# A decoder layer on one core: single rows' products and value products issued in unbroken groups, and the single rows of two projections' second halves moved behind the first row block

## The chip, the cores and the metric

The kernel runs on one core of a Trainium2 chip. A core has a matrix engine (TensorE, PE in the profile), whose weight loads are shown apart (PEld), a vector engine (VectorE, DVE), a scalar engine (ScalarE, ACT), a general engine (GpSimd, POOL) and an engine that here only issues transfers (SyncE, SP). Each engine takes its own instructions strictly in the order in which they were written down for it; between engines there are semaphores. The metric is the device time of one execution in microseconds. Before the change it is 970.07 us (median of three, 969.19 to 971.19).

## The reference, cut to what matters

One layer of a hybrid decoder serves a prompt of 512 rows and a group of 32 single rows (8 sequences of 4 tokens) with the same weights. The prompt attends to itself; the single rows attend to cached tokens and to cached memory of their own.

```python
h = rms_norm(x, g_mix_pre); z = h @ w_in             # mixer: 4 mLSTM heads, 4 differential attention heads
...
x = x + rms_norm(mix @ w_out, g_mix_post)
x = x + rms_norm(mem_attend(rms_norm(x, g_mem_pre), mk, mv, w_mq, w_mo), g_mem_post)   # 256 memory tokens
f, conv_new = conv_ffn(rms_norm(x, g_ffn_pre), conv_buf, w_up, w_dw, b_dw, w_down)     # gated MLP
x = x + rms_norm(f, g_ffn_post)
...
past_k = cache_dk[l][page_table]; past_v = cache_dv[l][page_table]   # single rows: 256 cached tokens each
ys, ... = layer(ys, pos_s, attend_s, ..., cache_mem_k[l], cache_mem_v[l], ...)
```

The model width is 1024, there are 4 heads of 256 in the attention to memory, and the MLP is 2752 wide.

## The kernel before, in words

The 544 rows are four row blocks b0 to b3 of 128 prompt rows and a fifth block, called 4 in the code, of the 32 single rows. All is float32; the big products of the prompt rows take their operands split into a high part (a cast on ACT, L142) and a low part (what the cast lost, a subtraction on DVE or POOL, L143), and three matmuls for each product: high by high (L387), high rows by low weights (L388), low rows by high weights (L389).

The single rows use full float32 in one product instead. A block of 32 rows fills 32 of the array's 128 columns, so `sample_mm` (L367) issues four matmuls at a time into four column groups that run side by side, each on other rows of the weights or on other output columns. It reads the weights from the staging tile in which they came from memory (`wst`, six buffers), not from the split copy (`wslot`, four slots). The profile counts two records for each such float32 matmul. The products of the single rows with cached memory and cached tokens work in the same way: scores against memory (`ssc`, L1396), values of cached tokens (`ops`, L1251), values of memory (`pso`, L1413); there each column group is a head.

A slot and its staging tile live as follows. SP loads 512 KB into `wst`; ACT casts it into the slot's high half as soon as the slot is free, and DVE then makes the low half. A staging tile can be loaded again only when both the split and the single rows' product have read it.

Two projections, `w_out` and `w_mo`, are computed in two halves of 512 output columns each (`proj_add`). The second half goes block by block with all four slots held (`block_major` in `gemmA`): one block takes 8 products of three matmuls. When a block is done, its row sums of squares, its scaling and its addition to the residual follow (`ev1`), its result is written to memory, and the next block's old residual `xb` is loaded. In the half-way point of each block, `mid` may transpose an earlier block's normalised rows (tile `tp`) into the next matmul's operand (`hqT` behind `w_out`, `fT` behind `w_mo`).

The program is traced once in Python; a scheduler then sets the order in which each engine gets its instructions, by dependences, its own cost model and priorities. So instructions that stand together in the code can be pulled apart: those of the single rows serve as filling wherever the scheduler believes that nothing else is ready. `tc.issue_after(x)` puts a block's instructions behind x on x's engine, and `tc.high_priority()` lets the scheduler prefer them.

Names in the prediction: "singles" are the 16 matmuls (32 records) that the single rows take for one half of a projection; a "run" is a number of column-group matmuls with nothing else of PE between them.

Of the kernel before, what the change touches and what calls it, by code (L numbers as in the profile page):

```python
# [1 line left out]

# [13 lines left out]
P = 128  # L16
DM = 1024
SEQ = 512
NB = 8
TS = 4  # L20
NS = NB * TS
ROWS = SEQ + NS
H = 4
# [50 lines left out]
def kernel(ctx: ExitStack, tc: tile.TileContext, I, O):  # L74
# [38 lines left out]
    def mmp(name="mm"):  # L113
        return psm.tile([P, 512], F32, name=name, tag="mm")
# [11 lines left out]
    mm = nc.tensor.matmul  # L126
# [200 lines left out]

    allb = [0, 1, 2, 3, 4]

    class Fill:  # L330


# [42 lines left out]
    def gemmA(xt, nk, blocks, evac, block_major=False, before=None, mid=None):  # L375


        ps = {}

        def one(b, k, s):  # L380
            if b == 4:
                if k % 2 == 0:
                    sample_mm(ps[b], [xt.sam(k), xt.sam(k + 1)], s[1], k == 0, k == nk - 2)
                return
            s, kk = s[0], k % 2
            c0, n = rows(b)
            mm(ps[b], lhsT=xt.hi(k, c0, c0 + n), rhs=s[:, 0, kk, :], start=(k == 0), stop=False)  # L387
            mm(ps[b], lhsT=xt.hi(k, c0, c0 + n), rhs=s[:, 1, kk, :], start=False, stop=False)  # L388
            mm(ps[b], lhsT=xt.lo(k, c0, c0 + n), rhs=s[:, 0, kk, :], start=False, stop=(k == nk - 1))  # L389

        if block_major:
            slots = [W.get() for _ in range((nk + 1) // 2)]
            for b in blocks:
                if before:
                    before(b)
                ps[b] = mmp()
                for k in range(nk):
                    if k == MIDK and mid:
                        mid()
                    one(b, k, slots[k // 2])  # L400
                    if b == blocks[-1] and k % 2 == 1:
                        W.free()
                evac(b, ps[b])
                yield 5.1
        else:
            for b in blocks:
                ps[b] = mmp()
            behind = []
            for k in range(nk):
                if k % 2 == 0:  # L410
                    s = W.get()
                    if 4 in blocks:
                        behind.append((k, s))
                for b in blocks:
                    if b < 4:
                        one(b, k, s)
# [211 lines left out]
    for c0, c1 in HALF:  # L628
        n = c1 - c0
        ps = mmp()  # L630
# [436 lines left out]
    def proj_add(xt, gname, src, gname2, dst, order=None, scale=None):  # L1067
# [173 lines left out]
    vts = {}  # L1241
# [4 lines left out]
            gather("cache_dv", b, g, st[:, 512 * g:512 * g + 512])  # L1246

    def dv_out(b):
        for g in range(2):
            for h in range(H):  # L1250
                mm(ops[NS * h:NS * h + NS, :P], lhsT=az[g][:, h, b * NS:(b + 1) * NS],  # L1251
                   rhs=vts[b][:, g * 512 + h * P:g * 512 + (h + 1) * P], start=(b == 0 and g == 0), stop=False)

    for t, _ in enumerate(pipe(NB, dv_load, lambda b: None, dv_out)):
        if t % 2 == 0:
# [133 lines left out]
            (VCP if q else nc.scalar.copy)(out=kts[b][:, 4 * q:4 * q + 4, c * P:(c + 1) * P], in_=v2(ps, P))  # L1389
        return t.ins  # L1390

    def mk_scores(b):
        ps = mmp("ssc")[:, :256]
        for c in range(2):
            for h in range(H):
                t = mm(ps[NS * h:NS * h + NS], lhsT=qs[:, 2 * h + c], rhs=kts[b][:, 2 * h + c, :], start=(c == 0), stop=(c == 1))  # L1396
        sample_exp(sall, b, ps, nm, su)
        return t.ins

    def mv_load(b):  # L1400

# [5 lines left out]
        for c in range(2):  # L1407
            dma(out=vts[b][c], in_=I["cache_mem_v"][0, b, c * P:(c + 1) * P].rearrange("t h d -> t (h d)"))

    def mv_out(b):  # L1410
        for c in range(2):
            for h in range(H):
                t = mm(pso[NS * h:NS * h + NS], lhsT=az[c][:, h, b * NS:(b + 1) * NS], rhs=vts[b][c][:, 256 * h:256 * h + 256],  # L1413
                       start=(b == 0 and c == 0), stop=(b == NB - 1 and c == 1))
        return t.ins

    sall = S([P, NB, 256], F32, "cas")
    nm, su = small(NB, "snm"), small(NB, "ssu")
# [8 lines left out]
                mk_load(j + 6)  # L1427

    next(prompt)
    for b in range(4):  # L1430
        t = mk_scores(b)
    with tc.issue_after(t):
        for j in range(8, 16):
            t = mk_turn(j)
# [5 lines left out]
        mv_load(b)  # L1440
    next(prompt)
    with tc.issue_after(t):
        for b in range(4, NB):
            t = mk_scores(b)
    for b in range(3, 7):
        mv_load(b)
    next(prompt)
# [4 lines left out]
    for n0 in (0, 512):  # L1452
        slotsA(w_mo, n0)
    W.nslots = NSLOT
    for b in range(4):
        mv_out(b)
        if b == 0:
            mv_load(7)
    W.pump()
    next(prompt, None)  # L1460
    next(prompt, None)
    for b in range(4, NB):
        mv_out(b)
    run(prompt)
    oS = Z("oS")[:, :256]
    nc.scalar.copy(out=oS, in_=pso)
# [357 lines left out]
```

## Time and profile before

| | |
|---|---|
| median of three runs | 970.07 us |
| profiled execution | 968.01 us, of which 966.2 us are its span |
| mean granted TensorE clock | 0.989 of full speed |
| PE busy | 940.1 us of the span |
| ACT, DVE, POOL busy | 388.0, 598.6 and 202.6 us |

The profile is one execution. In a timeline a row gives the start, the duration, engine, line, operation, output and inputs; "x8" says that eight neighbouring records of one kind are put together, and the bracket at its end how long the engine stood idle before it and what ended the wait. On PE, neighbouring matmuls overlap in the records, so that the distance from one start to the next tells what a matmul costs, not its duration.

### The profile page before, as it was taken

What the parts mean: (1) busy time and instruction counts of PE and PEld (TensorE: products, weight loads), DVE (VectorE), ACT (ScalarE), POOL (GpSimd) and SP (SyncE); (2) the same over time, 40 slices, a digit from 0 to 9 for tenths busy, and PEclk for the clock granted to TensorE, in tenths of its full rate; (3) what the DMA queues carried; (4) which work ended last, traced back from release to release, by engine and by line L of the source; (5) the groups of instructions that cost most, each with busy time, mean ns of one, the idle gap of its engine ahead of it and who ended that gap; (6) DMA issues with size and microseconds to landing.
All of it is one profiled execution on the core that took longest, in us unless ns stands there. A gap on an engine that the chain in (4) does not pass through costs nothing.

```text
span 966.2 us, 17070 instructions
## 1 busy us (share of the span) xinstructions
PE 940.1 (97%) x6615; PEld 813.3 (84%) x6615; DVE 598.6 (62%) x1127; ACT 388.0 (40%) x746; POOL 202.6 (21%) x397
## 2 busy tenths in 40 slices
PE   8999999999999999999999799999999999999994
PEld 5999787779866788998767699989988997997983
DVE  6835145555786367625554759827758675675677
ACT  6744134343686367534533524332212222222232
POOL 6610000016332124200000544301110110110114
PEclk9999999999999999999999999999999999999997
DMA  9950024344835359846734844063053303503213
GB/s 303 299 160 1 1 88 134 88 126 133 256 100 173 133 180 322 258 144 209 287 133 128 229 138 128 4 174 89 5 142 79 120 25 91 150 25 90 86 48 114
DMA packets 120529, 130.27 MB, mean 135 GB/s; under 512 B 8551, under 2 KB 85960, under 8 KB 120448
## 3 DMA queue, kind: packets, MB, share of 16 engines
q1 hardware_dynamic: 114264, 125.69, 41.9%
q10 hardware_dynamic: 6184, 3.48, 1.2%
q8 instruction: 52, 0.85, 0.4%
q14 instruction: 29, 0.24, 0.1%
HBM read 112.22 MB, written 16.93 MB: 134 GB/s over the span
## 4 chain that ended last, share of the span: by engine, by line
PE 86%; DVE 4%; DMA 4%; ACT 2%; POOL 2%; issue 1%; SPq 0%; DVEq 0%; POOLq 0%; ACTq 0%
PE mm L451 32%; PE mm L439 8%; PE mm L387 6%; PE mm L389 6%; PE mm L388 6%; PE mm L1660 4%; PE mm L1659 4%; PE mm L1658 4%; PE mm L367 2%; PE tpk L1388 1%; PE sda L1183 1%; DMA xb<-in_x_prompt_dram 1%; DMA wst<-in_w_mo_dram 1%; PE sca L1339 1%; DVE wslot L143 1%
## 5 line engine op out<-in xcount | busy, mean ns | idle before, releaser
L451 PEld LDWEIGHTS mm<-fT,wslot 128*128 128x128 f32 x1872 | 234.3, 188 | 2.1 <-issue 1.2
L451 PE MATMUL mm<-fT,wslot 128*128 128x256 f32 (+1 forms) x1872 | 236.0, 288 | 0.0
L142 ACT CAST wslot<-wst 128x1024 fp32r<-128x1024 f32 x125 | 131.1, 1051 | 254.7 <-PE mm L451 76.0
L143 DVE TENSOR_TENSOR wslot<-wst,wslot 128x1024 fp32r<-128x1024 f32 x125 | 155.7, 1249 | 90.9 <-ACT wslot L142 90.9
L1659 PE MATMUL mm<-wslot,act 128*128 128x512 f32 x176 | 69.6, 396 | 0.0
L1660 PE MATMUL mm<-wslot,act 128*128 128x512 f32 x176 | 68.9, 397 | 0.0
L1658 PE MATMUL mm<-wslot,act 128*128 128x512 f32 x176 | 68.7, 392 | 0.0
L1565 POOL COPY cvo<-u 128x2 f32<-128x2 f32 x43 | 15.2, 354 | 201.2 <-DVE u L1563 191.2
L387 PE MATMUL mm<-wslot,hT 128*128 128x512 f32 x128 | 52.2, 408 | 0.0
L388 PE MATMUL mm<-wslot,hT 128*128 128x512 f32 x128 | 51.3, 401 | 0.0
L389 PE MATMUL mm<-wslot,hT 128*128 128x512 f32 x128 | 51.3, 402 | 0.0
L1560 DVE TENSOR_TENSOR u<-mm,rsb 128x256 f32<-128x256 f32 x43 | 18.2, 424 | 52.9 <-PE mm L451 50.9
L451 PE MATMUL mm<-hT,wslot 128*128 128x256 f32 (+1 forms) x384 | 51.0, 289 | 0.0
L451 PEld LDWEIGHTS mm<-hT,wslot 128*128 128x128 f32 x384 | 49.2, 188 | 0.8 <-issue 0.4
L1658 PEld LDWEIGHTS mm<-wslot,act 128*128 128x128 f32 x176 | 33.6, 191 | 8.6 <-issue 0.8
L1659 PEld LDWEIGHTS mm<-wslot,act 128*128 128x128 f32 x176 | 33.1, 188 | 7.2
L1660 PEld LDWEIGHTS mm<-wslot,act 128*128 128x128 f32 x176 | 33.1, 188 | 7.2
L1577 ACT ACTIVATE c<-c 128x560 f32<-128x560 f32 x21 | 14.1, 672 | 54.9 <-DVE c L1571 51.6
L1571 DVE SCALAR_TENSOR_TENSOR c<-u,cvT,c 128x560 f32<-128x560 f32 x43 | 34.2, 796 | 0.8
L1570 DVE SCALAR_TENSOR_TENSOR c<-u,cvT,c 128x560 f32<-128x560 f32 x43 | 34.1, 792 | 0.1
L439 PE MATMUL mm<-fT,wslot 128*128 128x256 f32 (+1 forms) x192 | 27.2, 303 | 2.6 <-POOL fT L143 2.4
L1671 DVE TENSOR_TENSOR yp<-mm,yp 128x512 f32<-128x512 f32 x40 | 27.1, 687 | 3.9 <-PE mm L1660 3.8
(469 smaller groups left out, 1868.3 us busy)
## 6 DMA issues: line engine op xcount, KB each, us to landing
wst<-in_w_up_dram SPq DMA_DIRECT2D x42, 512.0 KB
wst<-in_w_in_dram SPq DMA_DIRECT2D x28, 512.0 KB
wst<-in_w_down_dram SPq DMA_DIRECT2D x20, 512.0 KB
wst<-in_cache_mem_k_dram SPq DMA_DIRECT2D x16, 512.0 KB
wst<-in_w_mk_dram SPq DMA_DIRECT2D x8, 512.0 KB
xb<-in_x_prompt_dram SPq DMA_DIRECT2D x8, 512.0 KB
wst<-in_cache_dk_dram SPq DMA_DIRECT2D x16, 256.0 KB
wst<-in_cache_dv_dram SPq DMA_DIRECT2D x16, 256.0 KB
```

The lines of the kernel that those rows point to most:

```text
L142: nc.scalar.copy(out=hi, in_=src)
L143: (eng or nc.vector).tensor_tensor(out=lo, in0=src, in1=f32(hi), op=SUB)
L387: mm(ps[b], lhsT=xt.hi(k, c0, c0 + n), rhs=s[:, 0, kk, :], start=(k == 0), stop=False)
L388: mm(ps[b], lhsT=xt.hi(k, c0, c0 + n), rhs=s[:, 1, kk, :], start=False, stop=False)
L389: mm(ps[b], lhsT=xt.lo(k, c0, c0 + n), rhs=s[:, 0, kk, :], start=False, stop=(k == nk - 1))
L439: mm(ps, lhsT=s[:, l, k, :], rhs=x(k, c0, c1), start=(k == 0 and j == 0), stop=(k == 7 and j == 2))
L451: mm(ps[i], lhsT=s[:, l, k, :], rhs=x(k, c0, c1), start=(k == 0 and j == 0), stop=(k == 7 and j == 2))
L1570: STT(out=c, in0=u[:, 1:EXT - 1], scalar=w[1], in1=c, op0=MUL, op1=ADD)
L1571: STT(out=c, in0=u[:, 0:EXT - 2], scalar=w[0], in1=c, op0=MUL, op1=ADD)
L1658: mm(ps, lhsT=t[:, 0, c0:c0 + P], rhs=s[:, 0, i % 2, :], start=st, stop=False)
L1659: mm(ps, lhsT=t[:, 0, c0:c0 + P], rhs=s[:, 1, i % 2, :], start=False, stop=False)
L1660: return mm(ps, lhsT=t[:, 1, c0:c0 + P], rhs=s[:, 0, i % 2, :], start=False, stop=en)
```

## The change

A small context manager `burst(ins)` is added: nothing for `None`, otherwise behind `ins` on its engine with high priority. With it

- the singles are issued behind the last row block's last product in the plain form of `gemmA`, and behind the previous block's last product in its block-major form;
- the second halves of `w_out` and `w_mo` go in the order b0, 4, b1, b2, b3 instead of 4, b0, b1, b2, b3 (and the loads of `xb` with them);
- the value products over cached tokens (`dv_out`) are issued for two sequences at a time, each behind the one before;
- the scores (`mk_scores`) and the value products (`mv_out`) over cached memory are chained in the same way, the latter in pairs for the second four sequences.

```diff
+    @contextmanager
+    def burst(ins):
+        if ins is None:
+            yield
+        else:
+            with tc.issue_after(ins), tc.high_priority():
+                yield
...
         if block_major:
             slots = [W.get() for _ in range((nk + 1) // 2)]
+            t = None
             for b in blocks:
                 if before:
                     before(b)
                 ps[b] = mmp()
+                if b == 4 and t is not None:
+                    with burst(t.ins):
+                        for k in range(nk):
+                            one(b, k, slots[k // 2])
+                    evac(b, ps[b])
+                    yield 2.1
+                    continue
                 for k in range(nk):
                     if k == MIDK and mid:
                         mid()
-                    one(b, k, slots[k // 2])
+                    t = one(b, k, slots[k // 2])
...
             if behind:
-                for k, s in behind:
-                    one(4, k, s)
+                with burst(t.ins):
+                    for k, s in behind:
+                        one(4, k, s)
                 evac(4, ps[4])
...
-            run(gemmA(xt, 8, [4, 0, 1, 2, 3], ev1, block_major=True, before=before, mid=mid))
+            run(gemmA(xt, 8, [0, 4, 1, 2, 3], ev1, block_major=True, before=before, mid=mid))
...
     def dv_out(b):
-        for g in range(2):
-            for h in range(H):
-                mm(ops[NS * h:NS * h + NS, :P], lhsT=az[g][:, h, b * NS:(b + 1) * NS],
-                   rhs=vts[b][:, g * 512 + h * P:g * 512 + (h + 1) * P], start=(b == 0 and g == 0), stop=False)
+        if b % 2 == 0:
+            return
+        t = None
+        for b in (b - 1, b):
+            for g in range(2):
+                for h in range(H):
+                    with burst(t):
+                        t = mm(ops[NS * h:NS * h + NS, :P], lhsT=az[g][:, h, b * NS:(b + 1) * NS],
+                               rhs=vts[b][:, g * 512 + h * P:g * 512 + (h + 1) * P], start=(b == 0 and g == 0), stop=False).ins
...
-    def mk_scores(b):
+    def mk_scores(b, t=None):
         ps = mmp("ssc")[:, :256]
         for c in range(2):
             for h in range(H):
-                t = mm(ps[NS * h:NS * h + NS], lhsT=qs[:, 2 * h + c], rhs=kts[b][:, 2 * h + c, :], start=(c == 0), stop=(c == 1))
+                with burst(t):
+                    t = mm(ps[NS * h:NS * h + NS], lhsT=qs[:, 2 * h + c], rhs=kts[b][:, 2 * h + c, :], start=(c == 0),
+                           stop=(c == 1)).ins
...
-    def mv_out(b):
+    def mv_out(b, t=None):
         for c in range(2):
             for h in range(H):
-                t = mm(pso[NS * h:NS * h + NS], lhsT=az[c][:, h, b * NS:(b + 1) * NS], rhs=vts[b][c][:, 256 * h:256 * h + 256],
-                       start=(b == 0 and c == 0), stop=(b == NB - 1 and c == 1))
-        return t.ins
+                with burst(t):
+                    t = mm(pso[NS * h:NS * h + NS], lhsT=az[c][:, h, b * NS:(b + 1) * NS],
+                           rhs=vts[b][c][:, 256 * h:256 * h + 256], start=(b == 0 and c == 0), stop=(b == NB - 1 and c == 1)).ins
+        return t
...
-    for b in range(4, NB):
-        mv_out(b)
+    for b in range(4, NB, 2):
+        mv_out(b + 1, mv_out(b))
```

Every engine issues the same instructions as before, in another order; 29 lines are added, so that L387 to L389 become L396 to L398, L367 becomes L376, L1054 L1072 and L1413 L1439. The order shows it at three places of PE.

The first place is the value products over cached memory, ahead of `w_mo`. Between them stand the prompt's own attention to memory: scores (`sca`), transposes (`cpt`) and value products (`cpo`). Before:

```order
L1413 MATMUL pso<-wst,caz 32x256
L1357 MATMUL cpt<-cpk,cp 128x128 x3
L1413 MATMUL pso<-wst,caz 32x256 x23
L1413 MATMUL pso<-vt,caz 32x256 x8
L1357 MATMUL cpt<-cpk,cp 128x128 x4
...
L1413 MATMUL pso<-vt,caz 32x256 x9
L1369 MATMUL cpo<-pT,mvN 128x512 x2
L1413 MATMUL pso<-vt,caz 32x256 x2
L1369 MATMUL cpo<-pT,mvN 128x512 x6
L1413 MATMUL pso<-vt,caz 32x256 x6
```

and now:

```order
L1439 MATMUL pso<-wst,caz 32x256 x24
L1439 MATMUL pso<-vt,caz 32x256 x8
L1380 MATMUL cpt<-cpk,cp 128x128 x7
...
L1439 MATMUL pso<-vt,caz 32x256 x16
L1392 MATMUL cpo<-pT,mvN 128x512 x8
L1439 MATMUL pso<-vt,caz 32x256 x8
L1439 MATMUL pso<-wst,caz 32x256 x8
```

Six runs of 1, 31, 9, 2, 6 and 15 matmuls have become three of 32, 16 and 16.

The second place is the passage from the first half of `w_out` to the second. `mm_3904` is the first half's block b3, whose products run over slots 3670, 3675, 3680 and 3685; 3912, 3923, 3934 and 3945 are the second half's slots; `dat` is the transpose of the attention's last row block, from which `mixT01` and `mixT11` (high and low part of the operand's second half) get their last columns. Before, from b3's fourth product on (`mm_3967` are the singles, `mm_4009` is b0, `mm_4055` b1):

```order
L389 MATMUL mm_3904<-wslot_3675,mixT10_2788 128x512
L367 MATMUL mm_3967<-wst_3911,xts_2551 32x256 x4
L367 MATMUL mm_3967<-wst_3922,xts_2551 32x256 x4
L367 MATMUL mm_3967<-wst_3933,xts_2551 32x256 x4
L1054 MATMUL dat_3869<-cpk_87,dasq_3861 128x128 x4
L367 MATMUL mm_3967<-wst_3944,xts_2551 32x256 x4
L387 MATMUL mm_4009<-wslot_3912,mixT00_2787 128x512
L387 MATMUL mm_4055<-wslot_3912,mixT00_2787 128x512
...
L389 MATMUL mm_4055<-wslot_3923,mixT10_2788 128x512
L387 MATMUL mm_3904<-wslot_3680,mixT01_3110 128x512
```

and now (`mm_3967` is b0; the singles follow as a run of 16 behind its last product):

```order
L398 MATMUL mm_3904<-wslot_3675,mixT10_2788 128x512
L1072 MATMUL dat_3869<-cpk_87,dasq_3861 128x128 x4
L396 MATMUL mm_3967<-wslot_3912,mixT00_2787 128x512
...
L398 MATMUL mm_3967<-wslot_3923,mixT10_2788 128x512
L396 MATMUL mm_3904<-wslot_3680,mixT01_3110 128x512
...
L398 MATMUL mm_3904<-wslot_3685,mixT11_3111 128x512
L396 MATMUL mm_3967<-wslot_3934,mixT01_3110 128x512
```

Between `dat` and b3's fifth product there stood one group of singles, 12 matmuls of b0 and 12 of b1; now there stand the 12 of b0. Slots 3934 and 3945 were first read some 12 matmuls of b2 after b3's end, and are now read by the next matmul.

The third place is the same passage of `w_mo`. `mm_5819` are the first half's singles; 5844 (slot 5845), 5873 (5874), 5902 (5903) and 5931 (5932) are the second half's staging tiles and slots. Before (`mm_5983` singles, `mm_6026` b0, `mm_6073` b1):

```order
L367 MATMUL mm_5819<-wst_5627,xts_4727 32x256 x4
L367 MATMUL mm_5983<-wst_5844,xts_4727 32x256 x4
L367 MATMUL mm_5983<-wst_5873,xts_4727 32x256 x4
L387 MATMUL mm_6026<-wslot_5845,oT00_5443 128x512
...
L389 MATMUL mm_6026<-wslot_5874,oT10_5444 128x512
L387 MATMUL mm_6073<-wslot_5845,oT00_5443 128x512
...
L387 MATMUL mm_6073<-wslot_5874,oT00_5443 128x512
L367 MATMUL mm_5983<-wst_5902,xts_4727 32x256 x4
L388 MATMUL mm_6073<-wslot_5874,oT00_5443 128x512
L387 MATMUL mm_6026<-wslot_5903,oT01_5670 128x512
```

and now (`mm_5983` is b0):

```order
L376 MATMUL mm_5819<-wst_5627,xts_4727 32x256 x4
L396 MATMUL mm_5983<-wslot_5845,oT00_5443 128x512
...
L398 MATMUL mm_5983<-wslot_5874,oT10_5444 128x512
L396 MATMUL mm_5983<-wslot_5903,oT01_5670 128x512
```

Two groups of singles, seven matmuls of b1 and a third group stood between the first halves' end and slot 5903 beside b0's 12 matmuls; now only these 12 stand there.

More of the change, by code (lines that the diff above doesn't have):

```diff
@@ L1 @@
-from contextlib import ExitStack
+from contextlib import ExitStack, contextmanager
 import concourse.bass as bass
@@ L388, in one @@
             mm(ps[b], lhsT=xt.hi(k, c0, c0 + n), rhs=s[:, 1, kk, :], start=False, stop=False)
-            mm(ps[b], lhsT=xt.lo(k, c0, c0 + n), rhs=s[:, 0, kk, :], start=False, stop=(k == nk - 1))
+            return mm(ps[b], lhsT=xt.lo(k, c0, c0 + n), rhs=s[:, 0, kk, :], start=False, stop=(k == nk - 1))
         if block_major:
             slots = [W.get() for _ in range((nk + 1) // 2)]
+            t = None
             for b in blocks:
@@ L407, in gemmA @@
                 ps[b] = mmp()
-            behind = []
+            behind, t = [], None
             for k in range(nk):
@@ L415, in gemmA @@
                     if b < 4:
-                        one(b, k, s)
+                        t = one(b, k, s)
                 if k % 2 == 1:
@@ L1408, in mv_load @@
             dma(out=vts[b][c], in_=I["cache_mem_v"][0, b, c * P:(c + 1) * P].rearrange("t h d -> t (h d)"))
[L1410 removed]
+    def mv_out(b, t=None):
         for c in range(2):
             for h in range(H):
[L1413 to L1415 removed]
+                with burst(t):
+                    t = mm(pso[NS * h:NS * h + NS], lhsT=az[c][:, h, b * NS:(b + 1) * NS],
+                           rhs=vts[b][c][:, 256 * h:256 * h + 256], start=(b == 0 and c == 0), stop=(b == NB - 1 and c == 1)).ins
+        return t
     sall = S([P, NB, 256], F32, "cas")
@@ L1429 @@
     next(prompt)
+    t = None
     for b in range(4):
-        t = mk_scores(b)
+        t = mk_scores(b, t)
     with tc.issue_after(t):
@@ L1442 @@
     with tc.issue_after(t):
+        t = None
         for b in range(4, NB):
-            t = mk_scores(b)
+            t = mk_scores(b, t)
     for b in range(3, 7):
@@ L1454 @@
     W.nslots = NSLOT
+    t = None
     for b in range(4):
-        mv_out(b)
+        t = mv_out(b, t)
         if b == 0:
```

1 line of the change is left out of this document (removed).

## The prediction

> **What bounds the kernel now.** I read the busy shares, the chain, PE's list of waits, and then PE's timeline where the order changes.
>
> ```profile
> PE 940.1 (97%) x6615; PEld 813.3 (84%) x6615; DVE 598.6 (62%) x1127; ACT 388.0 (40%) x746; POOL 202.6 (21%) x397
> PE 86%; DVE 4%; DMA 4%; ACT 2%; POOL 2%; issue 1%; SPq 0%; DVEq 0%; POOLq 0%; ACTq 0%
> PE mm L439 <- POOL fT L143: 2.4, 1, 2.4
> PE rsb L1533 <- DVE ht L320: 2.3, 1, 2.3
> PE tpk L1163 <- ACT numS L965: 1.1, 1, 1.1
> PE tp L318 <- ACT hN L306: 0.9, 1, 0.9
> PE ost L1469 <- ACT oS L1466: 0.8, 1, 0.8
> ```
>
> PE bounds: busy 97% of the span, 86% of the chain, with five single waits around the changed places (line, releaser, total, times, longest). So a shorter PE sequence is a shorter kernel, as long as no new wait appears; where PE did not wait, the trace does not show how close it came. The profiled execution took 968.01 us (span 966.2 and 1.8 around it), 2.06 under the median of 970.07; the sum is a difference made on that execution and is then put on the median.
>
> **What a run costs.** Two places in `w_in`, an unbroken batch of singles and a broken one:
>
> ```profile
> 118.57 0.39 PE L388 MATMUL mm<-wslot,hT 128*128 128x512 f32 x1
> 118.80 0.40 PE L389 MATMUL mm<-wslot,hT 128*128 128x512 f32 x1
> 119.13 1.93 PE L367 MATMUL mm<-wst,xts 128*32 128x256 f32 x32
> 120.99 0.50 PE L787 MATMUL mld<-mlE,ones_r 128*128 128x512 f32 x1
> 178.91 0.63 PE L367 MATMUL mm<-wst,xts 128*32 128x256 f32 x4
> 179.47 0.71 PE L856 MATMUL mli<-Cst,qT 128*128 128x129 f32 x4
> 180.11 0.64 PE L367 MATMUL mm<-wst,xts 128*32 128x256 f32 x8
> 180.68 0.71 PE L863 MATMUL mln<-vN,mlD 128*128 128x129 f32 x4
> 181.77 1.49 PE L367 MATMUL mm<-wst,xts 128*32 128x256 f32 x20
> 183.19 0.50 PE L387 MATMUL mm<-wslot,hT 128*128 128x512 f32 x1
> 183.53 0.60 PE L838 MATMUL mlu<-vN,wk 128*128 128x129 f32 x4
> ```
>
> From start to start, a 512-wide product costs 0.23; before a run it is 0.33, and the one behind it 0.34 (183.19 to 183.53): about 0.2 for each run. An unbroken batch of 16 matmuls takes 1.86 (119.13 to 120.99). The broken one takes 0.56, 0.57 and 1.42, together 2.55: two matmuls cost what four do, since the four column groups run side by side and a quarter of them leaves the rest empty; each group begun costs about 0.43 (1.42 − 0.57, over two more groups).
>
> In the new order the `w_in` batches of 2, 4, 10 and of 3, 13 matmuls become two of 16. Groups: 1+1+3 and 1+4, now 4 and 4, two fewer; runs: three fewer. By the prices of groups and runs that is 2 × 0.43 + 3 × 0.2 = 1.46; by the timeline's own 2.55 − 1.86 and two runs the first batch alone gives 1.09, and the second a group and a run, 0.63. I take the latter, −1.7, since it was measured whole. The values of cached tokens go from runs of 11, 13, 16, 16, 8 to four of 16, one run and one group (half as long at 128 columns) fewer: −0.4. The singles of `w_out` go from 16, 12, 4 to 16, 16 and those of `w_mo` from 24, 4, 4 to 16, 16: one run fewer each, −0.3 each with what the short ones overpay (0.57 for 0.43). The scores over memory go from runs of 5, 27, 32 to 26, 6, 32: nothing. The values of memory:
>
> ```profile
> 476.16 0.62 PE L1413 MATMUL pso<-wst,caz 128*32 128x256 f32 x2
> 477.19 2.58 PE L1413 MATMUL pso<-wst,caz 128*32 128x256 f32 x43
> 482.77 1.48 PE L1413 MATMUL pso<-vt,caz 128*32 128x256 f32 x18
> 486.98 1.06 PE L1413 MATMUL pso<-vt,caz 128*32 128x256 f32 x12
> 491.39 1.07 ACT L142 CAST wslot<-wst 128x1024 fp32r<-128x1024 f32 x1
> GB/s 126 126 239 391 378 240 113 76 101 227 328 359 303 321 315 296 315 347 328 334 359 315 328 359 397 410 416 410 397 347 221 195 132 19 0 50 0 0 0 0
> ```
>
> Runs of 1, 31, 9, 2, 6, 15 matmuls are 1+8+3+1+2+4 = 19 groups; 32, 16, 16 are 16: 3 × 0.43 + 3 × 0.2 = −1.9. But behind them `ost` waits for the copy `oS` (0.8 above, ending at 492.8), and in ACT's new order the cast of `w_mo`'s fourth slot stands right ahead of that copy. Its tile lands when the transfers end: the last row is the rate from 479 to 492 us in 40 slices of 0.325, which drops to 19 in the 34th, that begins at 489.7. With the cast at 490.1 (0.95 to the next start), it ends at 491.1, and `ost`, which came 1.4 behind that cast's start, comes at 491.5 instead of 492.8: −1.3 of the −1.9 arrives.
>
> At the end of `w_in`, ACT now takes a second exponential (0.46, one such with its accumulator) ahead of the copy `numS` for which PE waited 1.1: +0.46.
>
> ```profile
> 252.17 0.38 ACT L1187 ACTIVATE pda<-sda,nm 128x128 f32<-128x128 f32 x1
> 252.43 0.21 ACT L1187 ACTIVATION_READ_ACCUMULATOR pda<-sda,nm 128x1 f32 x1
> ```
>
> **`w_out`, first half to second.** Here PE did not wait. Before:
>
> ```profile
> 326.49 1.93 PE L367 MATMUL mm<-wst,xts 128*32 128x256 f32 x32
> 330.05 1.05 ACT L142 CAST wslot<-wst 128x1024 fp32r<-128x1024 f32 x1 [2.37 <-PE mm L389]
> 334.42 1.05 ACT L142 CAST memT<-wst 128x1024 fp32r<-128x1024 f32 x1 [1.93 <-DMA wst<-mem_d]
> 336.74 0.61 ACT L142 CAST mixT<-dtm 128x512 fp32r<-128x512 f32 x1
> 331.13 1.23 DVE L143 TENSOR_TENSOR wslot<-wst,wslot 128x1024 fp32r<-128x1024 f32 x1 [2.73 <-ACT wslot L142]
> 337.43 2.04 POOL L143 TENSOR_TENSOR mixT<-dtm,mixT 128x512 fp32r<-128x512 f32 x1 [6.53 <-ACT mixT L142]
> ```
>
> A slot takes 1.05 and 1.23 after its release, so products of low weights (L397) come 2.3 behind it. The 16 singles and the 24 matmuls of b0 and b1 (5.6 at 0.23) covered all of it. Now b3's four products end at 331.2 and `dat` at 331.9. L397 on slot 3912 waits until 332.4, 0.2. DVE puts `dtm` (0.7) between the two slots, so 3923 is whole at 334.2 and L397 waits 0.5. b0's 12 end at 335.5. b3's next needs `mixT`'s cast; ACT has the `memT` cast ahead of it, whose tile lands at 334.4 whatever PE does, so `mixT` is done at 336.1: 0.6. Its low part on POOL is done at 338.1: L398 waits 1.6. b3 ends at 340.5. Slot 3934 is free when b3 has read slot 3680 for the last time, at 339.3; it is whole at 341.6 and is read at once: 0.9; slot 3945 behind it 0.4. Together **+4.2**. The singles now hold their staging tiles until b0's end; the loads that queue behind that on SP are `w_mv`'s, first needed some 20 later, which hides them.
>
> Some comes back: the wait for `hN` (0.9 above) ends a chain of `xb` loads, each issued behind its predecessor's addition; in SP's new order b3's load stands behind three fewer weight loads. I let the wait go: −0.9. The bounds for the stage: nothing kept (−0.6, if casts start earlier than I place them), and +4.2 with no recovery.
>
> **`w_mo`, first half to second.**
>
> ```profile
> 519.34 2.80 PE L367 MATMUL mm<-wst,xts 128*32 128x256 f32 x48
> 524.13 1.05 ACT L142 CAST wslot<-wst 128x1024 fp32r<-128x1024 f32 x1 [1.59 <-DMA wst<-in_w_mo_dram]
> 525.22 1.22 DVE L143 TENSOR_TENSOR wslot<-wst,wslot 128x1024 fp32r<-128x1024 f32 x1 [2.22 <-ACT wslot L142]
> 526.97 1.21 DVE L143 TENSOR_TENSOR wslot<-wst,wslot 128x1024 fp32r<-128x1024 f32 x1
> 552.01 5.19 POOL L143 TENSOR_TENSOR fT<-ht,fT 128x512 fp32r<-128x512 f32 x3
> 549.00:552.60 3.60, 1.11 (x8) 0.91 (x8) 3.60 (x7) 2.89 (x6) 3.44 (x7) 1.00 0.99 291
> 552.60:556.00 3.40, 0.97 (x6) 0.68 (x5) 3.40 (x5) 0.00 (x0) 3.40 (x3) 0.50 1.16 306
> 556.00:559.40 3.40, 3.40 (x18) 3.40 (x18) 2.15 (x4) 1.15 (x2) 1.46 (x3) 0.50 1.05 345
> ```
>
> The third slot's tile comes from memory at 524.1, since its staging tile is freed by the first half's singles. Now 16 singles (1.86) and b0's 12 matmuls are through at 524.0; the high part is there at 525.2, the low at 526.4 (waits of 1.1 and 1.0), the fourth slot's low at 528.2 (0.3): +2.4, less 0.3. But the stage ends on another chain: `fT`'s low parts on POOL, of which PE waited for the second (552.01 + 2 × 1.73). b0's two parts now leave POOL early, and only b1's two are behind b1's transposes, which come 2.1 later; POOL is through its first at about 555.1 by my count, against 555.5. So 0 for the stage; bounds +2.1 (the chain shifts whole) and −3.4: in the last two rows the granted clock is 0.50 for 6.8 us, half of which is lost, right behind a stretch with PE busy 1.11 of 3.60.
>
> **Sum.** −1.7 + 0.46 − 0.4 − 0.3 + 4.2 − 0.9 − 1.3 + 0 = +0.1, so 968.1 for the profiled execution and **970.2 us** on the median's basis: no change.
>
> **Rivals.** *The savings arrive.* −1.7 − 0.4 − 0.3 − 1.9 − 0.3 = −4.6, so 965.5; down to 962 if the slow clock at 552.6 goes too. For it: no wait at these places before. Against: an order without cover, and durations that don't depend on it.
>
> *Slot waits decide.* In `w_out` nothing is recovered (+4.2, not +3.3), `w_mo` keeps its 2.1, `ost` gains nothing (0 for −1.3): +0.1 + 0.9 + 2.1 + 1.3 = +4.4, so 974.5. It decides from the point where new waits exceed the 4.6 saved. Against: two of the three tails have another chain to run into.
>
> *Slow clock behind the new waits.* Rows above: 2.5 idle in 3.6 us was followed by the clock at half; `w_out` has 2.2 of idle between 335.5 and 338.1. One such stretch of 3.4 us costs 1.7: 971.9, and with the rival before 976.2. The Trainium skill ("TensorE: Matmul & The Clock Gate", What's actually happening) says that an idle window of about 3.4 us throttles the clock, by a window that runs freely; the two rows of 3.4 agree with its length, and how idle a window must be no row tells.
>
> *No fewer breaks.* The scores show that chaining does not always keep others out; but the order shows nine fewer runs, so I give it nothing of its own.
>
> **How the numbers follow.** Within 0.2% (1.9 us, about what a measurement of this kernel tells from no change): 0.38, its own range 968.2 to 972. Savings arrive: 0.27. Slower: 0.35, of which slot waits 0.22 and slow clock 0.13. The range goes from 964.8 to 975: it takes in most of the first and of the second rival.
>
> **What would show it.** The singles as eight runs of 32 records at 1.86; PE waits at L397 and L398 in `w_out` on DVE `wslot` and POOL `mixT` of some 4 us, in `w_mo` on ACT and DVE `wslot` of some 2; the wait on `hN` gone; L439's start in the fT stage near where it was. If PE waits for neither slots nor `mixT`, the forecast is wrong on the slow side; if L439 starts 2 later, on the fast side.

## The result and the profile after

The changed kernel takes 975.69 us (median of six, 974.93 to 980.33) against 969.62 for the kernel before in the same comparison: a ratio of 1.0066, 95% interval 1.0052 to 1.008. It is slower, by some 6 us; the forecast was 970.2, no change, with a range up to 975.0. The profiled execution has a span of 973.4, 7.2 more than before's 966.2.

PE is as busy as before (940.3 us for 940.1); what was added is idle time, 33.1 us of the span for 26.1. The list of what PE waited for (line, releaser, total, times, longest):

```profile
PE rsb L1562 <- DVE ht L320: 4.5, 1, 4.5
PE mm L397 <- DVE wslot L143: 2.2, 4, 0.8
PE ssc L1187 <- DVE kT L1182: 1.7, 1, 1.7
PE tpk L1181 <- ACT numS L983: 1.5, 1, 1.5
PE ost L1498 <- ACT oS L1495: 1.5, 1, 1.5
...
PE mm L398 <- POOL mixT L143: 1.1, 1, 1.1
...
PE mm L396 <- ACT wslot L142: 0.8, 1, 0.8
PE ssc L1420 <- DVE kT L1412: 0.8, 1, 0.8
```

The waits for slots (L396, L397) and for `mixT` (L398) are new, and so is the one for `kT` at L1420; the one for `kT` at L1187 has grown from 0.2 to 1.7, those for `numS` and `oS` by 0.4 and 0.7; the wait for `hN` is gone; the one for `ht` at the end of `w_mo` has grown from 2.3 to 4.5, while the 2.4 for `fT` behind it is gone.

Where the time came from, by stages: the distance from one landmark of PE to the next, in before's trace, and the differences to it in the traces of the change and of the experiments that this table is for. The landmarks are the first product of `w_in` that reads `hT`, the first `tpk`, the first singles of `w_out`, the first transpose of cached memory keys, the first `pso`, the first and the last product of `w_mo`, the first L451 product (L469 now) that reads `fT`, and PE's last instruction.

| stage | before | change | e1 | e2 | e3 | e4 | e11 | e12 |
|---|---|---|---|---|---|---|---|---|
| start | 94.89 | −0.45 | +0.73 | +1.30 | +0.55 | −0.55 | −0.59 | −0.07 |
| `w_in`, mLSTM | 157.44 | −1.31 | −1.30 | −1.51 | −2.74 | −2.74 | −2.73 | −1.50 |
| attention | 74.16 | +1.79 | +1.21 | +0.10 | +2.25 | +1.21 | +1.87 | +0.12 |
| `w_out` second half to `w_mq` | 90.11 | +4.21 | +0.43 | +5.13 | +0.34 | +3.32 | +0.04 | −0.86 |
| keys and scores of memory | 59.56 | +0.87 | +0.88 | −0.02 | +0.90 | +0.92 | +0.87 | −0.02 |
| values of memory | 18.09 | −0.61 | −1.35 | +0.18 | −0.41 | −0.85 | −1.13 | −1.11 |
| `w_mo` | 53.16 | +2.20 | +0.04 | +3.38 | +2.18 | +3.25 | +3.14 | +4.45 |
| end of `w_mo`, first products of the MLP | 35.95 | +0.48 | +0.29 | +0.90 | −0.11 | −5.23 | −5.37 | −5.11 |
| rest | 369.69 | −0.02 | +0.07 | −0.01 | +0.02 | +0.02 | +0.01 | −0.03 |

The change's column adds up to +7.16. The two passages into second halves and their ends account for +6.9, attention and scores for +2.7, and −1.9 is what the groups save in `w_in` and in the values of memory; the start's −0.45 is none of the change's. In e4, e11 and e12 eight transposes `tp` (0.8 us) stand ahead of `w_mo`'s last product that stand behind it in the others: so much of their `w_mo` row has only moved there from the row behind it. The start varies by over a microsecond from execution to execution, and so does `w_in`, for a reason that stands at the end; so the medians, not single spans, decide below.

PE at the second half of `w_out`, from the timeline:

```profile
331.65 0.48 PE L396 MATMUL mm<-wslot,mixT 128*128 128x512 f32 x1
332.46 0.50 PE L397 MATMUL mm<-wslot,mixT 128*128 128x512 f32 x1 [0.32 <-DVE wslot L143]
...
335.77 0.51 PE L396 MATMUL mm<-wslot,mixT 128*128 128x512 f32 x1
336.12 0.39 PE L397 MATMUL mm<-wslot,mixT 128*128 128x512 f32 x1
337.64 0.50 PE L398 MATMUL mm<-wslot,mixT 128*128 128x512 f32 x1 [1.13 <-POOL mixT L143]
...
340.07 0.40 PE L396 MATMUL mm<-wslot,mixT 128*128 128x512 f32 x1
341.23 0.50 PE L397 MATMUL mm<-wslot,mixT 128*128 128x512 f32 x1 [0.76 <-DVE wslot L143]
```

The bracket gives the idle time, but the loss is the distance between starts less 0.23: 0.58, 1.29 and 0.93 at the three quoted stops. Each stop costs 0.16 to 0.26 more than its idle time: neighbouring products overlap by some 0.16 in the rows (0.39 long, 0.23 apart), and those on either side of a stop do not. The six stops of this passage add up to 3.6.

The end of `w_mo`, in the chain of waits, in order of time (start, duration, what):

```profile
536.57 1.43 DVE xb L1124 x2
538.02 1.16 ACT hN L299 x2
539.26 0.20 POOL rs L293
539.53 0.56 POOL rs L294
540.39 6.27 DMA xb<-x_d
546.75 1.41 DVE xb L1124 x2
548.18 0.32 SPq L1125
548.54 3.72 DMA xb<-x_d
552.63 0.40 issue
553.03 0.74 DVE xb L1124
...
556.96 2.53 DVE wslot L143 x2
559.49 0.60 DVE ht L320
```

The old residual of the single rows (128 KB) takes 6.27 us, that of a row block (512 KB) behind it 3.72. In the 6.27 us the transfers ran at 242 GB/s, which is some 1.5 MB, so most of it was other data. SP's rows ahead of that load, in the kernel before (there it is b0's, 512 KB, and its addition starts 4.05 behind the issue) and now:

```profile
528.98 1.62 SPq L247 DMA_DIRECT2D wst<-in_w_up_dram  x1
534.65 0.33 SPq L1107 DMA_DIRECT2D x_d<-xb  x1
535.03 0.42 SPq L1091 DMA_DIRECT2D xb<-x_d  x1
```

```profile
534.68 3.89 SPq L247 DMA_DIRECT2D wst<-in_w_up_dram  x4
538.61 1.73 SPq L1125 DMA_DIRECT2D x_d<-xb  x1
540.39 0.42 SPq L1109 DMA_DIRECT2D xb<-x_d  x1
```

### The profile page after: what moved, and what is told of

Same layout as the page of the kernel before. It is cut to its first block, busy times and chain, and to the rows that moved or that the text cites. A ratio compares the mean times of both kernels' runs of the same rounds, so it can differ in the third digit from the quotient of the medians.

```text
span 973.4 us, 17059 instructions
## 1 busy us (share of the span) xinstructions
PE 940.3 (97%) x6615; PEld 813.5 (84%) x6615; DVE 601.9 (62%) x1127; ACT 387.8 (40%) x746; POOL 201.6 (21%) x397
## 4 chain that ended last, share of the span: by engine, by line
PE 79%; DMA 9%; DVE 7%; ACT 2%; issue 2%; POOL 1%; SPq 0%; ACTq 0%; DVEq 0%; POOLq 0%
PE mm L469 31%; PE mm L457 6%; PE mm L398 5%; PE mm L396 5%; PE mm L397 5%; PE mm L1689 4%; PE mm L1688 4%; PE mm L1687 4%; DVE wslot L143 1%; DMA wst<-in_w_mo_dram 1%; PE mm L376 1%; PE sda L1201 1%; DVE xb L1124 1%; DMA xb<-x_d 1%; DMA xb<-in_x_prompt_dram 1%
## 5 line engine op out<-in xcount | busy, mean ns | idle before, releaser
L469 PE MATMUL mm<-fT,wslot 128*128 128x256 f32 (+1 forms) x1872 | 236.0, 288 | 0.0
L469 PEld LDWEIGHTS mm<-fT,wslot 128*128 128x128 f32 x1872 | 234.2, 188 | 2.1 <-issue 1.2
L396 PE MATMUL mm<-wslot,hT 128*128 128x512 f32 x128 | 52.3, 408 | 0.0
L398 PE MATMUL mm<-wslot,hT 128*128 128x512 f32 x128 | 51.5, 403 | 0.0
L397 PE MATMUL mm<-wslot,hT 128*128 128x512 f32 x128 | 51.2, 400 | 0.0
L469 PE MATMUL mm<-hT,wslot 128*128 128x256 f32 (+1 forms) x384 | 50.7, 289 | 0.0
L469 PEld LDWEIGHTS mm<-hT,wslot 128*128 128x128 f32 x384 | 49.1, 188 | 0.4
L1688 PEld LDWEIGHTS mm<-wslot,act 128*128 128x128 f32 x176 | 33.1, 188 | 7.3
L1689 PEld LDWEIGHTS mm<-wslot,act 128*128 128x128 f32 x176 | 33.1, 188 | 7.2
L398 PEld LDWEIGHTS mm<-wslot,hT 128*128 128x128 f32 x128 | 24.4, 191 | 5.2
```

What stands on the lines that cost most here:

```text
L398: return mm(ps[b], lhsT=xt.lo(k, c0, c0 + n), rhs=s[:, 0, kk, :], start=False, stop=(k == nk - 1))
L469: mm(ps[i], lhsT=s[:, l, k, :], rhs=x(k, c0, c1), start=(k == 0 and j == 0), stop=(k == 7 and j == 2))
L1688: mm(ps, lhsT=t[:, 0, c0:c0 + P], rhs=s[:, 1, i % 2, :], start=False, stop=False)
L1689: return mm(ps, lhsT=t[:, 1, c0:c0 + P], rhs=s[:, 0, i % 2, :], start=False, stop=en)
```

## The experiments

Theory A was that the new order of the second halves costs the time; its rival B, that the groups themselves do, by what they push back in other stages. Within A, theory C says that `w_mo`'s end is set by the loads of `xb`, against D, slot splits.

**e1, everything but the new order**

```diff
-            run(gemmA(xt, 8, [0, 4, 1, 2, 3], ev1, ...))
+            run(gemmA(xt, 8, [4, 0, 1, 2, 3], ev1, ...))
```

> Everything of the change is kept but the order of the second halves, which is 4, b0, b1, b2, b3 again in both projections. Theory A (the new order costs the time, as b0's products come to their slots before these are split): the 3.8 us that PE falls back from the first half of w_out to the second, and the 2.1 and 0.5 of w_mo and its end, go away: 975.7 - 6.4 = 969.3, about as before. Theory B (the unbroken groups themselves cost it, by what waits behind them in the attention and score stages): these stages stay as in the changed kernel, and at least 3 us of the loss of 6.1 remain: 972.5 or more.

Measured: 969.89 against 969.91, ratio 0.9996 (0.9977 to 1.0014). The loss is gone, as A said. In the table, `w_out` and `w_mo` are back, and the unbroken groups alone are a wash: −1.30 and −1.35 against +1.21 and +0.88. So the stages that B named do lose 2.1, but that is only what the groups save, and B's time, 972.5 or more, did not come.

**e2, the new order alone**

```diff
 before:
-            run(gemmA(xt, 8, [4, 0, 1, 2, 3], ev1, ...))
+            run(gemmA(xt, 8, [0, 4, 1, 2, 3], ev1, ...))   # with the burst of block 4 behind b0
```

> The kernel before with the second halves in the order b0, 4, b1, b2, b3 (single rows as a group behind b0), and nothing else of the change. Theory A: 969.6 + 3.8 + 2.6 = 976, slower than the whole change, since the savings of the value products and of w_in are missing. Theory B: 971 or less.

Measured: 977.19, ratio 1.0076 (1.0055 to 1.0098). The order costs some 7 us by itself, at least as much as the whole change (the two intervals overlap). Of the 3.38 in `w_mo`, some 1.2 is a stretch at half clock behind the slot stops, which the change's trace does not have; the last section shows it.

**e3, the new order in `w_mo` alone**

```diff
-            run(gemmA(xt, 8, [0, 4, 1, 2, 3], ev1, ...))
+            run(gemmA(xt, 8, [0, 4, 1, 2, 3] if scale is not None else [4, 0, 1, 2, 3], ev1, ...))
```

> The change, with the old order in the second half of w_out alone; w_mo keeps the new one. Theory A: the four waits on split slots and mixT between 331 and 343 us go (3.8 us), the end of w_mo stays late (wait of rsb for ht of 4.5): 971.9. Theory B: within 1 us of the changed kernel, 975 to 976.

Measured: 971.83, ratio 1.0019 (1.0002 to 1.0035). PE waits for no slot between the first half of `w_out` and `w_mq`; `w_out`'s stage is at +0.34 instead of +4.21, and `w_mo` keeps its loss.

**e4, the single rows' residual loaded ahead with b0's**

```diff
         def before(b):
-            n = rows(b)[1]
-            xb[b] = N("xb")[:n]
-            dma(out=xb[b], in_=src(b))
+            for b in ((0, 4) if b == 0 else () if b == 4 else (b,)):
+                n = rows(b)[1]
+                xb[b] = N("xb")[:n]
+                dma(out=xb[b], in_=src(b))
```

> The change, with the old residual of the single rows loaded together with that of b0, ahead of the second half, in both projections (a second buffer of the same pool instead of a load behind b0's addition). Theory C (at the end of w_mo the chain of residual loads decides: the single rows' load was issued at 540.4 behind four weight loads of 512 KB and its data came at 546.7, and b1's load, addition, ACT's pass over it and the three slot casts behind that pass follow): PE's wait of 4.5 us for ht at 560.1 shrinks by 2 to 4 us, 972 to 974. Rival D (the wait is for slot splits that can't begin before PE has freed the slots): the wait stays 4 to 5 us and the time 975 to 976.

Measured: 971.17, ratio 1.0012 (0.9995 to 1.0029), 4.5 below the change and somewhat better than the 972 to 974 expected. Theory C holds and D falls as the first cause. In e4's list of waits the largest of the change is down by 3.0:

```profile
PE rsb L1563 <- DVE ht L320: 1.5, 1, 1.5
```

and more was gained than the wait. Windows of 3.4 us at the end of `w_mo` (busy time of PE, PEld, DVE, ACT, POOL, granted clock, DMA share, GB/s), first of the change, then of e4:

```profile
555.80:559.20 3.40, 0.00 (x0) 0.00 (x0) 2.69 (x6) 3.02 (x5) 3.24 (x6) 1.00 0.98 308
559.20:562.60 3.40, 2.39 (x8) 1.93 (x9) 3.40 (x7) 1.72 (x4) 2.51 (x4) 0.64 0.93 241
562.60:566.00 3.40, 3.40 (x18) 3.40 (x17) 2.06 (x6) 0.55 (x2) 3.02 (x5) 0.50 1.08 379
```

```profile
551.40:554.80 3.40, 1.80 (x10) 1.32 (x9) 3.40 (x6) 2.42 (x6) 1.28 (x4) 1.00 0.75 203
554.80:558.20 3.40, 3.03 (x25) 2.75 (x25) 3.40 (x5) 1.31 (x3) 3.23 (x3) 1.00 1.06 371
```

Behind a stretch without any PE work the clock was at half; in the kernel before it was so behind one with PE busy 1.11 of 3.60. In e4 it stayed whole. The stage goes from +0.48 to −5.23: the wait's 3.0, the 0.8 of the moved transposes, and some 1.9 that is left for the slow clock.

**e5, only the singles of the plain form grouped**

```diff
 before:
             if behind:
-                for k, s in behind:
-                    one(4, k, s)
+                with burst(t.ins):
+                    for k, s in behind:
+                        one(4, k, s)
```

> The kernel before, with only the singles of the plain form (w_in, first half of w_mo) in unbroken groups; order of the second halves, cached tokens, scores and value products as before. By the changed kernel's trace: -1.3 us up to the first tpk at 250 us, and then +2 in the attention stage, where the scheduler has put 12 transposes tpk in a row and PE waits for mltm (0.4) and kT (1.7): together +0.7, 970.6. If instead the groups of cached tokens were what broke that stage, it stays as before and the time is 968.6.

Measured: 972.21, ratio 1.0016 (0.9999 to 1.0033): by times, not told from no change; the trace decides. The waits for `mltm` (0.4) and `kT` (1.7) are there, with cached tokens as before; so it is the grouping in `w_in` that makes the scheduler put the attention stage in another order. The time is 1.6 above the expectation: two more waits came, 1.9 for `pda` ahead of `w_out` and some 1.3 for `hqT` and `ql`, with the singles of `w_out`'s second half in one run of 16 for 12 and 4, which the edit does not touch.

**e6, only the values of cached memory grouped**

```diff
 before:
     def mv_out(b, t=None):
         for c in range(2):
             for h in range(H):
+                with burst(t):
...
-    for b in range(4, NB):
-        mv_out(b)
+    for b in range(4, NB, 2):
+        mv_out(b + 1, mv_out(b))
```

> The kernel before, with only the value products over cached memory in runs of 32, 16 and 16. Savings of broken groups 1.9 us, of which 1.3 arrive at ost: 968.6. If the wait for the fourth slot's cast and oS takes it all: 969.9, and the wait of ost grows from 0.8 to 2.7.

Measured: 969.64 against 970.3, ratio 0.9997 (0.9981 to 1.0013): by times, undecided. In its trace the way from the first `pso` to the first product of `w_mo` is 1.50 shorter; the wait of `ost` is 0.6, not 2.7.

**e7, the kernel before with the first two residual loads together**

```diff
 before:
         def before(b):
-            n = rows(b)[1]
-            ...
+            for b in ((4, 0) if b == 4 else () if b == 0 else (b,)):
+                n = rows(b)[1]
+                ...
```

> The kernel before, with b0's old residual loaded together with that of the single rows ahead of the second half, in both projections. If the chain of residual loads also sets the end of w_mo in the old order (PE's waits of 2.3 and 2.4 us around 551 and 555, and the 3.4 lost to the clock at half speed behind them), each later addition comes some 4 us earlier, and 3 to 8 us go: 962 to 967. If the end there is set by the slot splits on DVE and by POOL's three low parts (5.2 us), nothing changes: 969 to 971.

Measured: 968.23, ratio 0.9983 (0.9968 to 0.9998). Between the two expectations: the load chain did take part in the old order, but `ht` still waits 2.2 for DVE's slot splits, and only the wait for `fT` (2.4) went. The clock was at half from 552.62 to 559.45 as in the kernel before, now with PE busy 6.31 of these 6.83 us for 4.41; so the stage is only 1.33 shorter.

**e8, the diffs of e6 and e7 together**

> The two before in one: sum of both, by the first of each 961 to 966, and better than either kernel of the comparison.

Measured: 967.67, ratio 0.9974 (0.9962 to 0.9986): better than both kernels, but not as good as the 961 to 966 expected. The gain of e6 alone could not be told from no change, and that of e7 only just; together they are clear.

**e9, e8 with the values of cached tokens grouped too**

```diff
 e8:
+        if b % 2 == 0:
+            return
+        t = None
+        for b in (b - 1, b):
             for g in range(2):
                 for h in range(H):
+                    with burst(t):
```

> The kernel of e8 with the value products over cached tokens in four runs of 16 as well. The order of the attention stage ahead of them stays that of the kernel before. One run and one group fewer: -0.4, 967.3. If these groups cost the attention stage its waits for mltm and kT (0.4 and 1.7), 969 to 970.

Measured: 966.53, ratio 0.9966 (0.9953 to 0.9979). These groups bring no wait to the attention stage, which is 0.47 shorter than before's; in e8's trace it was 0.21 longer. The gain over e8 is not shown by the times: the intervals overlap.

**e10, only the scores over cached memory chained**

```diff
 before:
-    def mk_scores(b):
+    def mk_scores(b, t=None):
...
+                with burst(t):
```

> The kernel before, with only the scores over cached memory chained (runs of 26, 6, 32 for 5, 27, 32). If the chaining brings the wait of 0.8 us for kT ahead of the last 32 scores, that wait is there and the time is 970.8; if that wait comes from the changed kernel's lateness elsewhere, it is absent and the time 969.9.

Measured: 971.99, ratio 1.0023 (1.001 to 1.0037). The wait of 0.8 for `kT` is there, so the chaining brings it: 26 scores in a row now stand ahead of four of the transposes that make `kT`, where 5 did, and the 6 behind these wait for the copy. As in e5, the rest of the excess lies between `w_out` and `w_mq` (+2.45 there), where the scheduler moved what the edit does not touch.

**e11, the change with e3's and e4's edits**

```diff
+            pair = (0, 4) if scale is not None else (4, 0)      # the order of each projection's first two
+            for b in (pair if b == pair[0] else () if b == pair[1] else (b,)):
```

> The whole change with two parts taken away: the old order in w_out's second half, and the first two residual loads together in both projections. If the four waits in w_out (3.8 us, e3) and the load chain at the end of w_mo (4.5 us, e4) are separate causes, both go: 975.7 - 3.9 - 4.5 = 967.3. If they are one (lateness of the first showing up at the second), the time stays at 971, as with either alone.

Measured: 966.66 against 969.91, ratio 0.9967 (0.9955 to 0.9979). The two are separate causes and add up: 3.9 and 4.5 were expected, 9.0 came.

**e12, the parts that the runs speak for**

e11 without `burst` at the singles of the plain form and without the chaining of the scores over cached memory.

```diff
 e11:
             if behind:
-                with burst(t.ins):
+                with burst(None):
...
-                with burst(t):
-                    t = mm(ps[NS * h:NS * h + NS], lhsT=qs[:, 2 * h + c], ...)
+                t = mm(ps[NS * h:NS * h + NS], lhsT=qs[:, 2 * h + c], ...)
```

> The parts that stood their trial, together: values of cached tokens and of cached memory in runs, the new order in w_mo alone, and the first two residual loads together in both projections; w_in's singles, the scores and w_out's second half as in the kernel before. From e11 to this, the attention stage's waits (2.1), the scores' (0.8) go and the saving in w_in (1.3) is lost: 966.7 - 1.6 = 965.1. If the new order costs w_mo its waits on slots (1.6) and these are not paid back by the shorter end of the stage, it is no better than e9, 966.5.

Measured: 965.89 against 970.56, ratio 0.995 (0.9933 to 0.9968), 9.8 below the change's 975.69 and faster than the kernel before by 0.3 to 0.7%. It lies between the two expectations, so whether the new order in `w_mo` belongs to the kept parts stays open. `w_mo` takes 4.45 more up to its last product (0.8 of it the moved transposes, and 1.3 more than in e11, behind a stretch at half clock), and its end 5.11 less: −0.66 together. In e9, with the old order, the two are at +0.07 and −1.58: −1.51 together. The intervals of e9 and e12 overlap.

## Why the prediction was wrong

Point by point, in microseconds:

| step of the prediction | forecast | measured in the trace |
|---|---|---|
| groups in `w_in`, with the longer wait for `numS` | −1.2 | −1.31 |
| groups of cached tokens, the attention stage | −0.4 | +1.79 |
| `w_out`, waits for slots and `mixT` | +4.2 − 0.3 | +3.6 over six stops, without the −0.3 |
| wait for `hN` let go | −0.9 | gone, but two new stops (0.4 idle each); stage +4.21 in all |
| scores over memory | 0 | +0.87 |
| values of memory | −1.3 | −0.61 |
| `w_mo` and its end | 0 | +2.20 and +0.48 |

**What held.** The price of broken groups: the batch in `w_in` that took 2.55 is now one row, and its next instruction starts 1.86 later.

```profile
178.53 1.93 PE L376 MATMUL mm<-wst,xts 128*32 128x256 f32 x32
180.39 0.71 PE L874 MATMUL mli<-Cst,qT 128*128 128x129 f32 x4
```

The waits in `w_out` came where they were put, one by one: 0.2, 0.5, 0.6, 1.6, 0.9, 0.4 forecast, and 0.58, 0.24, 0.31, 1.29, 0.93, 0.22 lost. For the three largest the profile names what ended them, and it is what was forecast; the other three are too short for that. So did those in `w_mo` on ACT's and DVE's slot halves (+2.4 − 0.3 forecast, +2.20 found), and e1 and e2 show that the order makes them.

Beyond their forecasts are `w_mo` with its end by 2.7, the attention stage by 2.2, `w_out` by 1.2, the scores by 0.9 and the values by 0.7.

**The step that failed** is "So 0 for the stage" at the end of `w_mo`: I let the lateness of 2.1 vanish in the wait that follows, and +2.20 and +0.48 were measured. I held that POOL's low parts of `fT` end the stage, and that two of them leave POOL early. They did leave early, and PE's wait for POOL is gone. But I took the tail's other chain to stay where it was, and it moved too, by two things that I had not followed. First, the singles keep the second half's staging tiles until b0 is done, as I wrote of `w_out`; in `w_mo` the loads behind them are `w_up`'s (SP waits 7.9 for the singles, until 534.68), and four of these were issued in a bunch right ahead of `xb`'s. The residual of the single rows then took 6.27. That the bunch makes it so long is read from the rows; no run moves the `w_up` loads alone. "The loads that queue behind that on SP" counted only as late loads, not as loads in another's way. Second, b1's addition hangs on that chain (it comes at 552.4, not at 545.8 as before), ACT's pass over the sum (`hN`) hangs on the addition, ACT's three slot casts stand behind that pass, DVE's three low halves behind the casts, and b1's `ht` behind them on DVE. The addition in the kernel before, then the rows now:

```profile
545.82 1.40 DVE L1106 SCALAR_TENSOR_TENSOR xb<-y,rs,xb 128x512 f32<-128x512 f32 x2
```

```profile
552.36 1.41 DVE L1124 SCALAR_TENSOR_TENSOR xb<-y,rs,xb 128x512 f32<-128x512 f32 x2 [1.62 <-DMA xb<-x_d]
...
556.96 2.53 DVE L143 TENSOR_TENSOR wslot<-wst,wslot 128x1024 fp32r<-128x1024 f32 x2
559.41 0.68 DVE L320 TENSOR_TENSOR ht<-tp,gT 128x512 f32<-128x512 f32 x1
```

```profile
553.86 1.06 ACT L299 ACTIVATE hN<-xb 128x1024 f32<-128x1024 f32 x1 [3.01 <-DVE xb L1124]
...
555.30 2.94 ACT L142 CAST wslot<-wst 128x1024 fp32r<-128x1024 f32 x3
```

e4 takes the first link away, and `w_mo` with its end is 4.66 shorter than in the change (+3.25 − 5.23 for +2.20 + 0.48), as the times say (4.5).

**The second** is that I priced the attention stage by its broken groups alone. PE's order there had changed 25 us ahead of them, and I looked at the rows of the singles only:

```profile
260.00 0.66 PE L1181 MATMUL tpk<-cpk,wst 128*128 128x128 f32 x4 [0.41 <-DVE mltm L1016]
...
261.53 1.48 PE L1181 MATMUL tpk<-cpk,wst 128*128 128x128 f32 x12
264.68 0.65 PE L1187 MATMUL ssc<-kT,qz 128*32 128x260 f32 x8 [1.67 <-DVE kT L1182]
```

Twelve transposes in a row, then scores that need their copies: DVE comes to the copy only at 263.86, behind other work, and the scores wait 1.7 for it:

```profile
263.86 1.27 DVE L1182 COPY kT<-tpk 128x512 f32<-128x512 f32 x2
```

Before, scores and other products stood between the transposes. e5 shows that the groups in `w_in` bring this order, and e9 that those of the cached tokens do not. The scores over memory, which I gave "nothing", lost 0.87 by a wait of the same kind. Together this is 3.1 against me.

The values of memory gained 0.61 of the 1.3: the wait of `ost` grew to 1.5, and one of 0.4 for `pT` came behind it. In e1, where the wait of `ost` stayed at 0.8, they gained 1.35.

The rival that I called "slot waits decide", at 974.5, was the nearest in mechanism: its place in both projections is what came. But it took `w_mo`'s lateness for 2.1 and no more, it lacked the attention stage, and the values gained 0.61 where it gave nothing; that its sum came within 1.2 of the time is in part luck. So is the 976.2 of the slow clock on top of it, which is nearer still: in the change's `w_out` the clock stayed whole. Cut where the clock's own windows begin (the last section shows them), the most idle one there has PE busy 2.14 of 3.42:

```profile
334.89:338.31 3.42, 2.14 (x9) 1.14 (x8) 2.83 (x2) 2.15 (x4) 1.78 (x1) 1.00 0.18 44
```

Of the rule that I cited from the Trainium skill ("TensorE: Matmul & The Clock Gate", What's actually happening), that an idle window of about 3.4 us throttles the clock, the traces bear out the length, and that a window need not be empty: 0.03 of 3.41 (the change, 556.76) and 1.12 (the kernel before, 549.21) did it, 2.14 did not; the last section has those between.

The bound of −3.4 in the prediction was too wide: of the 6.8 us at half clock in the kernel before, PE was busy for 4.41 only, so that at most some 2.2 were lost there.

## What to carry to other kernels

Filling that looks like waste on the bound engine may be what covers a chain elsewhere: before closing a gap in an in-order queue, name what becomes due at once and where its operands are by then. Follow a lateness through to the end of the stage on every engine, with the loads that it bunches up in front of others on a shared queue; a wait "that is there anyway" absorbs a delay only if the chain behind it does not start from the thing that is delayed. And where a scheduler sets the order, a local edit is to be read in the order of the whole program: more than a third of this loss (2.7 of 7.2) lay in stages whose code the order of the second halves does not touch, or that no edit touched.

## What the runs showed of the hardware that I had not expected

A slow clock can follow work, not only idle time. At 92 to 96 us PE runs a row of matmuls of 4 and 8 output columns (`dps`, 1.9 us); PE counts as busy all through, and in seven of the fourteen traces the next 3.4 us run at half clock. The kernel before, and e2 with the same PE order up to there:

```profile
91.82:95.23 3.41, 3.41 (x28) 3.14 (x28) 1.71 (x4) 1.62 (x3) 0.00 (x0) 1.00 0.00 0
95.23:98.65 3.42, 3.42 (x16) 2.36 (x15) 0.16 (x1) 0.00 (x0) 0.00 (x0) 0.50 0.00 0
```

```profile
91.40:94.81 3.41, 3.41 (x30) 3.20 (x28) 0.29 (x2) 1.07 (x2) 0.00 (x0) 1.00 0.02 5
94.81:98.22 3.41, 3.41 (x28) 2.82 (x29) 1.53 (x3) 0.54 (x2) 0.00 (x0) 1.00 0.00 0
```

What goes with it is where the row falls. In each trace all changes of the granted clock lie whole multiples of 3.413 us apart (in the kernel before at 95.23, 98.65, 552.62 and 559.45), as if they marked windows that run through the execution; the rows above are cut there. In the seven traces with the slow stretch (before, the change, e1, e6, e7, e9, e10) the whole row lies in one window (before: 93.02 to 94.89); in the seven without it a window ends inside the row (e2: at 94.81, in 94.31 to 96.19). No run moves the row on purpose.

Cut in this way from 13 to 945 us, every window at full clock with PE busy 1.46 us or less was followed by half clock, and none with more than 1.90 but that of the row. Between 1.70 and 1.90 both came. The two slot stops of `w_mo` in the new order are such a case: they were followed by half clock in e2 and e12,

```profile
528.31:531.72 3.41, 1.77 (x7) 0.93 (x6) 1.46 (x2) 2.54 (x4) 0.00 (x0) 1.00 1.05 338
531.72:535.13 3.41, 3.41 (x9) 2.63 (x10) 1.49 (x2) 0.07 (x1) 0.00 (x0) 0.50 0.53 135
```

```profile
520.35:523.76 3.41, 1.71 (x7) 0.87 (x6) 1.94 (x3) 2.60 (x4) 0.00 (x0) 1.00 1.05 328
523.76:527.18 3.42, 3.42 (x10) 2.49 (x8) 1.01 (x1) 0.00 (x0) 0.00 (x0) 0.50 0.39 99
```

but not in e3 (1.81 of 3.41), nor in the change, e4 and e11, where they fall into two windows. So the rival of the slow clock was real, in the other projection and in some executions.

In the table, `w_in` is shorter by 1.5 in e2 and e12, whose edits leave it alone, and by 2.7 instead of 1.3 in e3, e4 and e11, whose edits are the change's there: these are the traces without the slow stretch at 95 us. That is a difference as large as what this change saves anywhere, and it takes medians of several executions to see past it.
